# Softmax attention with 256-column products of P and V, and an output projection with two kept weight tiles and another order of PSUM banks

## The chip, the cores and the metric

One core of one Trainium2 chip. The metric is the device time of one execution in microseconds (us), lower is better. The unchanged kernel takes 2593.43 us, the median of 3 runs (2592.44 to 2593.51).

## The reference

Two layers over 1040 frames (16 learned ones and 1024 inputs) of width 1024. In each layer a normalised input goes through one projection into a group of linear-attention heads (GLA) and a group of eight softmax heads (FoX). The two groups' outputs, 512 columns each, go through one output projection and are added to the residual; a gated feed-forward part with a short convolution follows. The two places that the change touches, cut to what is computed:

```python
logits = einsum('bqhd,bkhd->bhqk', q_b, kf) + c_b[..., None] - c_k[:, :, None, :]
logits = where(key_pos <= q_pos, logits, -inf)
o = einsum('bhqk,bkhd->bqhd', softmax(logits, axis=-1), vf)          # FoX, per block of queries
...
h = h + concatenate([o_gla, o_fox], axis=-1) @ w_out[i]              # output projection
h = h + conv_ffn(rms_norm(h, ffn_norm[i]), ...)
```

## The kernel before

Activations lie transposed: eight tiles of 128 channels by 1040 frames. Every large product is made three times (`mm3`, L214): operand and weight are each split into a high part (rounded by a cast on ScalarE) and a low part (the difference, on VectorE), and high·high, low·high and high·low are summed in PSUM. A weight tile is loaded and split by `weights` (L170): for each four blocks of 128 rows one load on SP's queue (L179), one cast on ACT (L185) and one subtraction on DVE (L187; on POOL while the attention runs).

**Softmax attention.** Queries and keys are cut into nine tiles, the first of 112 frames and the others of 116 (`rows_of`, `start_of`). The work goes in steps of one head and one query tile; query tiles are grouped (7, 8), (5, 6), (3, 4), (1, 2), (0). A step makes scores S (L654, L655), the row maximum on DVE (L657) and P by an exponential on ACT (L669). Two steps later P is transposed on PE (L690), four key tiles to a PSUM tile `tr`, and split into PT (ACT L332, DVE L333). When both query tiles of a group are there, `fox_av` (L693) multiplies: V of one key tile, high and low part beside each other, is the weight (128 columns), and the two query tiles of PT, 2 x 116 = 232 columns, are what streams through; a key tile that only the later query tile sees has 116 columns. PT is stored as key tile, high or low part, 232 queries. Between the steps PE is given products of other projections as filler (`Work`); the tile framework's scheduler then orders each engine's list.

**Output projection.** The first four of the eight output tiles get seven eighths of their sum as filler of the attention. The rest is done in `ffn_up` by `wout` (L1098), where PE's order is the program's: for each half h of the frames (520 columns, in two products of 260) eight positions i, at each one output tile m out of `orders` (L1079). For h = 1 the tiles are 0, 4, 1, 5, 2, 6, 3, 7. Tiles 0 to 3 need one block of 128 rows (6 products), tiles 4 to 7 all eight (48 products). `stream` (L206) splits each position's weights while the position before is multiplied; so the weights of tiles 4 to 7 are loaded and split twice, once in each half. The sums lie in PSUM pairs of banks p0 to p3, taken by i % 4. DVE reads each sum out (L1110) and adds the residual, ACT squares it, DVE sums the squares (L1117). In the second half the scale of the first half is made after position 1: PE adds up the squares in p3 (`ssq`, L1086), DVE reads p3 (L1089), ACT and DVE form a reciprocal root (L273 to L277). The scaled first half is then written as operands x of the up projection (L1094, cast L1052, difference L1053) on the same two engines. `ensure` (L1071) splits the first five weight operands of the up projection (L1028, L1029) at the last position of h = 1. The up projection `up` follows, with sums and differences of operands; the second half's scale (again `ssq` in p3) stands after its first block of products.

Of the kernel before, what the change touches and what calls it, by code (L numbers as in the profile page):

```python
# [11 lines left out]
F32R = mybir.dt.float32r  # L12
# [12 lines left out]
KD = D // 128  # L25
# [8 lines left out]
FT, NT, FIRST = 116, 9, 112  # L34
# [5 lines left out]
M_GK, M_GQ, M_GV, M_GR, M_REM, M_FQ, M_FK, M_FV, M_WO, M_UP = 0, 2, 4, 8, 12, 13, 17, 21, 25, 33  # L40
# [11 lines left out]
NSPLIT = 4  # L52
# [82 lines left out]
class Kern:  # L135
# [31 lines left out]
        return self.vec[rows, o:o + 1]  # L167


    def weights(self, src, slots=None):  # L170
        nc = self.nc
        nk = src.shape[1]
        parts = []
        if slots:
            HI, LO = slots
        for k0 in range(0, nk, 4):
            n = min(4, nk - k0)
            raw = self.wp.tile([128, 4, 128], F32, tag="raw", name="raw", bufs=4)
            nc.sync.dma_start(raw[:, :n, :], src[:, k0:k0 + n, :])  # L179
            if slots:  # L180
                hi, lo = HI[:, k0:k0 + 4, :], LO[:, k0:k0 + 4, :]
            else:
                hi = self.wp.tile([128, 4, 128], F32R, tag="hi", name="hi")
                lo = self.wp.tile([128, 4, 128], F32R, tag="lo", name="lo")
            nc.scalar.copy(hi[:, :n, :], raw[:, :n, :])  # L185
            eng = nc.gpsimd if self.att else nc.vector
            eng.tensor_tensor(out=lo[:, :n, :], in0=raw[:, :n, :], in1=hi[:, :n, :].bitcast(F32), op=ALU.subtract)  # L187
            for k in range(n):
                parts.append((hi[:, k, :], lo[:, k, :]))
        return parts  # L190
# [485 lines left out]
    def fox_transposes(self, i, ci, P, PT, qoff, pp):  # L676
        nc = self.nc
        rows = self.rows_of(i)
        id_ = self.ident[:rows, :rows]
        tr = pp.tile([128, 4, 128], F32, tag="S" if ci == 2 else "tr", name="tr")  # L680
        qs = slice(qoff, qoff + rows)
        if ci == 2:
            nc.tensor.transpose(tr[:FT, 0, :FT], P[:FT, :FT], id_)
            self.split(PT[2][:, 0, :], PT[2][:, 1, :], tr[:FT, 0, :FT])
            return
        nt = min(4 * ci + 4, i + 1) - 4 * ci
        for j in range(nt):
            t = 4 * ci + j
            o, w = self.start_of(t) - self.start_of(4 * ci), FT if i else FIRST
            nc.tensor.transpose(tr[:w, j, :rows], P[:rows, o:o + w], id_)  # L690
        self.split(PT[ci][:w, :nt, 0, qs], PT[ci][:w, :nt, 1, qs], tr[:w, :nt, :rows])

    def fox_av(self, e, tiles, q, PT, avs, pp, part):  # L693
        nc = self.nc
        if part == 0:
            PT["av"] = pp.tile([128, 256], F32, tag="av", name="av")
        av = PT["av"]
        last = tiles[-1]
        width = FT * (len(tiles) - 1) + self.rows_of(last)
        for t in range(4 * part, min(4 * part + 4, last + 1)):  # L700
            a = 0 if t <= tiles[0] else FT
            for i in range(2):
                if t == NT - 1:
                    w, x = q["Vm"][:, e, :, :], PT[2][:, i, :]
                else:
                    r = self.rows_of(t)
                    w, x = q["V"][e][:r, t, :, :], PT[part][:r, t - 4 * part, i, a:width]
                nc.tensor.matmul(av[:, a:width], w.rearrange("p a b -> p (a b)"), x,  # L708
                                 start=(t == 0 and i == 0), stop=(t == last and i == 1))
        if last < 4 * part + 4:  # L710
            nc.scalar.copy(avs[:, e, :width], av[:, :width])

# [115 lines left out]
    def fox_schedule(self, lyr, at, n, p, e, ti, i, tiles, Ps, st, q, ap, pp, mix3):  # L828
        PT = st[e]

        def T_(ci, P):
            def f():
                if ti == len(tiles) - 1 and ci == 0:
                    for key in range(2):
                        PT[key] = ap.tile([FT, 4, 2, 2 * FT], F32R, tag=f"PT{key}", name=f"PT{key}", bufs=1)
                    if i == NT - 1:
                        PT[2] = ap.tile([FT, 2, FT], F32R, tag="PT2", name="PT2", bufs=1)
                self.fox_transposes(i, ci, P, PT, FT * ti, pp)
            return f
        for ci, P in enumerate(Ps):  # L840
            at(n + 2, f"T{ci}", T_(ci, P))
        if ti == len(tiles) - 1:
            PT["nch"] = len(Ps)
        if ti:
            return

        def av(ci):
            def f():
                if e == 0 and ci == 0:
                    one = len(tiles) == 1  # L850
                    st["avs"] = ap.tile([128, 2, FT if one else 2 * FT], F32, tag="av1" if one else "avs",
                                        name="avs", bufs=1)
                self.fox_av(e, tiles, q, PT, st["avs"], pp, ci)
            return f

        def fold():
            st["on"] = self.fox_fold(tiles, st["avs"], st["den"], ap, pp)

        def store():
            self.fox_store(lyr, p, tiles, st["on"], ap, pp, mix3() if p == 3 else None)  # L860
        for ci in range(PT["nch"]):
            at(n + 3, f"av{ci}", av(ci))
        if e == 1:
            at(n + 4, "fold", fold)
            at(n + 6, "store", store)
# [166 lines left out]
    def ffn_up(self, lyr, mix, hT, pp, fw, halves, o0, during_last):  # L1032
        nc, s = self.nc, self.slots
# [4 lines left out]
        bank2 = lambda name, i: pp.tile([128, 2, 512], F32, tag=f"p{i}", name=name, bufs=1)  # L1038
# [32 lines left out]
        def ensure(i):  # L1071
            while len(ops) < min(i + AHEAD + 1, len(seq)):
                ops.append(self.up_operand(lyr, *seq[len(ops)], fw, raws, len(ops) % 2))
# [5 lines left out]
        orders = [(4, 0, 5, 1, 6, 2, 7, 3), (0, 4, 1, 5, 2, 6, 3, 7)]  # L1079
        diff = lambda k: half(dd[k // 2], k % 2)  # L1080

        def scale(h):

            ps, r = bank2("ssq", 3), acc[:, sl[h]]
            for c in range(2):
                nc.tensor.matmul(ps[:, c, :n], self.ones[:], acc[:, halves[h] + c * n:halves[h] + c * n + n],  # L1086
                                 start=True, stop=True)
            vv, y0, a = half(tmp[0], 0), half(tmp[0], 1), half(tmp[1], 0)
            nc.vector.tensor_scalar(out=two(vv), in0=used(ps), scalar1=1.0 / D, scalar2=EPS, op0=ALU.mult, op1=ALU.add)  # L1089
            self.rsqrt(r, vv, y0, a)  # L1090
# [7 lines left out]
        def wout(i, h):  # L1098
            m = orders[h][i]
            k0 = KD - 1 if m < NSPLIT else 0  # L1100

            def f(w):
                if h == 1 and i == KD - 1:
                    ensure(0)
                ps = bank2("wo", i % 4)
                for k in range(len(w)):
                    for c in range(2):
                        self.mm3(ps[:, c, :n], w[k], mix[k0 + k], halves[h] + c * n, n, k == 0, k == len(w) - 1)
                x = hT[m][:, sl[h]]
                nc.vector.tensor_tensor(out=two(x), in0=used(ps), in1=two(x), op=ALU.add)  # L1110
                nc.gpsimd.dma_start(self.hm[m][:, sl[h]], x)
                if i == 0:
                    nc.scalar.activation(acc[:, sl[h]], x, AF.Square)
                else:
                    t = half(sq, i % 2)
                    nc.scalar.activation(t, x, AF.Square)
                    nc.vector.tensor_tensor(out=acc[:, sl[h]], in0=acc[:, sl[h]], in1=t, op=ALU.add)  # L1117
                if h == 0:
                    return
                if m < NSPLIT:  # L1120
                    nc.scalar.mul(half(gt, m % 2), x, gain(m))
                else:
                    nc.vector.scalar_tensor_tensor(out=diff(m - 4), in0=x, scalar=gain(m), in1=half(gt, m % 2),
                                                   op0=ALU.mult, op1=ALU.subtract)
                if i == 1:
                    scale(0)
                    operand(1)
                    operand(2)
                for k in turn.get(i, ()):
                    first_operand(k)  # L1130
            return (self.wm[lyr, M_WO + m][:, k0:KD, :], f)
        self.stream([wout(i, h) for h in range(2) for i in range(KD)])
        for x in mix:
            s.put(*x)
        s.put(gt)
# [93 lines left out]
        for i, (j, p) in enumerate(seq):  # L1229
# [3 lines left out]
            q = st.setdefault(j, {})  # L1233
# [3 lines left out]
            ps, w = q[bank], ops[i]  # L1237
# [452 lines left out]
```

## Time and profile before

| | |
|---|---|
| median of 3 runs | 2593.43 us |
| the profiled execution | 2591.4 us, of which the span is 2589.6 us |
| mean granted TensorE clock | 0.992 |
| busy share of the span | PE 96%, DVE 69%, ACT 50%, POOL 17% |
| products of P and V (`av`), layer 0, layer 1: first start, last start | 197.0, 524.1 us; 1474.1, 1800.8 us |
| products of the output projection in `ffn_up` (`wo`), layer 0, layer 1 | 538.9, 600.7 us; 1815.5, 1879.0 us |

The profile is of one execution. Times count from the start of the span. A row of the timeline has start, duration, engine, line, operation, what is written and read, and in brackets the idle time before it and what ended that. A matmul's duration has the way through the array in it, so the spacing of starts is what a product costs in a row of products. A row of the windows has, for one stretch, its length, each engine's busy time and number of instructions, the granted clock (PEclk), the DMA share and GB/s. A group row has busy time, mean ns of one, and idle time before. A row of the waits has total us, times, and the longest.

### The profile page before, as it was taken

How to read it: one execution, taken by the hardware profiler on the slowest of the kernel's cores; microseconds unless marked ns; L12 is line 12 of the kernel's file. 1: busy time of each engine (PE TensorE's matmuls, PEld its weight loads, DVE VectorE, ACT ScalarE, POOL GpSimd, SP SyncE). 2: the span in 40 equal slices, each digit the busy share in tenths (PEclk: the TensorE clock that was granted, in tenths of full speed). 3: DMA queues.
4: the chain of work that ended last, by engine and by line, in shares of the span. 5: the costliest groups of instructions: out<-in, count | busy, mean ns of one | idle time of the engine just before them, and what ended most of it. 6: DMA issues, size and time to landing. Idle time of an engine off the chain costs nothing.

```text
span 2589.6 us, 48743 instructions
## 1 busy us (share of the span) xinstructions
PE 2495.7 (96%) x19278; PEld 2424.9 (94%) x19278; DVE 1786.6 (69%) x3494; ACT 1288.4 (50%) x2745; POOL 432.6 (17%) x598
## 2 busy tenths in 40 slices
PE   8999999898999999999999999999999999999997
PEld 7988999898999999999999899998899999999997
DVE  7656776759877777853665666776697777777535
ACT  7336666635544445641443565665464444455312
POOL 4033334310000000100301233332100000001002
PEclk9999999999999999999999999999999999999998
DMA  3132134342322223863312222143423222257721
GB/s 125 65 89 60 51 93 127 109 145 89 110 75 87 79 79 129 200 165 107 110 50 67 72 78 76 57 146 114 148 70 114 78 74 86 76 162 179 196 61 67
DMA packets 119670, 263.03 MB, mean 102 GB/s; under 512 B 15008, under 2 KB 32672, under 8 KB 119440
## 3 DMA queue, kind: packets, MB, share of 16 engines
q1 hardware_dynamic: 95136, 184.89, 22.8%
q0 software_dynamic: 22432, 72.71, 10.1%
q8 instruction: 151, 2.47, 0.4%
q10 hardware_dynamic: 1872, 2.31, 0.3%
q14 instruction: 79, 0.65, 0.1%
HBM read 179.26 MB, written 67.81 MB: 95 GB/s over the span
## 4 chain that ended last, share of the span: by engine, by line
PE 62%; issue 16%; DVE 13%; ACT 4%; DMA 3%; POOL 1%; SPq 0%; DVEq 0%; POOLq 0%; ACTq 0%
PE mm L218 7%; PE mm L220 6%; PE mm L219 6%; PE up L218 5%; PE up L219 5%; PE up L220 5%; PE down L218 5%; PE down L219 5%; PE down L220 5%; PE av L708 2%; DVE S L657 2%; PE tr L690 2%; ACT P L669 1%; PE wo L218 1%; PE wo L219 1%
## 5 line engine op out<-in xcount | busy, mean ns | idle before, releaser
L218 PE MATMUL up<-x,hi 128*128 128x260 f32 (+1 forms) x2464 | 697.3, 283 | 2.3 <-ACT x L1052 1.6
L220 PE MATMUL up<-x,hi 128*128 128x260 f32 (+1 forms) x2464 | 695.8, 282 | 2.2 <-DVE x L1053 2.2
L219 PE MATMUL up<-x,lo 128*128 128x260 f32 (+1 forms) x2464 | 696.1, 283 | 0.8 <-DVE lo L1029 0.8
L220 PEld LDWEIGHTS up<-x,hi 128*128 128x128 f32 x2464 | 465.5, 189 | 3.1 <-DVE x L1053 3.1
L218 PEld LDWEIGHTS up<-x,hi 128*128 128x128 f32 x2464 | 464.4, 188 | 3.4 <-ACT x L1052 2.2
L219 PEld LDWEIGHTS up<-x,lo 128*128 128x128 f32 x2464 | 464.8, 189 | 1.0 <-DVE lo L1029 1.0
L1029 DVE TENSOR_TENSOR lo<-raw,hi 128x512 fp32r<-128x512 f32 x364 | 249.0, 689 | 171.3 <-ACT hi L1028 171.3
L218 PE MATMUL mm<-xh,hi 128*128 128x348 f32 (+4 forms) x1056 | 364.6, 345 | 0.0
L220 PE MATMUL mm<-xl,hi 128*128 128x348 f32 (+4 forms) x1056 | 340.1, 322 | 0.0
L219 PE MATMUL mm<-xh,lo 128*128 128x348 f32 (+4 forms) x1056 | 339.2, 321 | 0.0
L1028 ACT CAST hi<-raw 128x512 fp32r<-128x512 f32 x364 | 224.5, 620 | 145.0 <-PE up L220 87.4
L185 ACT CAST hi<-raw 128x512 fp32r<-128x512 f32 (+2 forms) x192 | 112.4, 587 | 201.4 <-PE down L220 114.2
L218 PEld LDWEIGHTS mm<-xh,hi 128*128 128x128 f32 x1056 | 200.2, 190 | 5.9 <-issue 5.3
L219 PEld LDWEIGHTS mm<-xh,lo 128*128 128x128 f32 x1056 | 200.1, 190 | 0.4 <-issue 0.3
L220 PEld LDWEIGHTS mm<-xl,hi 128*128 128x128 f32 x1056 | 198.9, 188 | 0.3 <-issue 0.3
L219 PE MATMUL down<-ah,lo 128*128 128x260 f32 (+1 forms) x704 | 198.6, 282 | 0.3 <-DVE lo L187 0.3
L220 PE MATMUL down<-al,hi 128*128 128x260 f32 (+1 forms) x704 | 198.3, 282 | 0.0
L218 PE MATMUL down<-ah,hi 128*128 128x260 f32 (+1 forms) x704 | 198.3, 282 | 0.0
L669 ACT ACTIVATE P<-S,m 116x460 f32<-116x460 f32 (+2 forms) x224 | 124.8, 561 | 100.1 <-DVE m L657 97.9
L333 DVE TENSOR_TENSOR PT<-tr,PT 116x464 fp32r<-116x464 f32 (+3 forms) x240 | 123.0, 516 | 63.2 <-ACT PT L332 62.3
L1222 POOL DMA_DIRECT2D actd<-cv x44 | 23.6, 535 | 763.5 <-DVE cv L1221 742.5
L1011 DVE TENSOR_TENSOR raw<-raw,raw 128x512 f32<-128x512 f32 x198 | 129.9, 689 | 22.4 <-DMA raw<-in_wd_dram 18.4
(276 smaller groups left out, 5901.0 us busy)
## 6 DMA issues: line engine op xcount, KB each, us to landing
raw<-in_wm_dram SPq DMA_DIRECT2D x338, 256.0 KB, 2.8
raw<-in_wd_dram SPq DMA_DIRECT2D x64, 256.0 KB, 3.5
actd<-cv POOLq DMA_DIRECT2D x22, 520.0 KB, 3.0
actd<-cv POOLq DMA_DIRECT2D x22, 512.0 KB, 3.0
cb<-cd SPq DMA_DIRECT2D x16, 520.0 KB, 3.8
st<-actd SPq DMA_DIRECT2D x14, 520.0 KB, 4.8
st<-actd SPq DMA_DIRECT2D x14, 512.0 KB, 5.3
kA<-kA SPq DMA_DIRECT2D x24, 260.0 KB, 4.3
```

Source lines behind the costliest of these rows:

```text
L185: nc.scalar.copy(hi[:, :n, :], raw[:, :n, :])
L218: nc.tensor.matmul(ps, wh, xh[:, c0:c0 + n], start=first, stop=False, skip_group_check=more)
L219: nc.tensor.matmul(ps, wl, xh[:, c0:c0 + n], start=False, stop=False, skip_group_check=more)
L220: nc.tensor.matmul(ps, wh, xl[:, c0:c0 + n], start=False, stop=last, skip_group_check=more)
L333: nc.vector.tensor_tensor(out=lo, in0=src, in1=hi.bitcast(F32), op=ALU.subtract)
L657: nc.vector.tensor_tensor_reduce(out=S[:rows, :n], in0=S[:rows, :n], in1=cb[:rows, c0:k1], scale=1.0, scalar=(BIG if ci == 0 else m[:rows, ...
L669: nc.scalar.activation(P[:rows, :n], S[:rows, :n], AF.Exp, scale=-1.0, bias=m[:rows, nch - 1:nch], accum_out=(den if nch == 1 else d3[:row ...
L690: nc.tensor.transpose(tr[:w, j, :rows], P[:rows, o:o + w], id_)
L708: nc.tensor.matmul(av[:, a:width], w.rearrange("p a b -> p (a b)"), x, start=(t == 0 and i == 0), stop=(t == last and i == 1))
L1011: nc.vector.tensor_tensor(out=q[out][:, :nk, :], in0=q[a][:, :nk, :], in1=q[b][:, :nk, :], op=op)
L1028: nc.scalar.copy(hi[:, :nk, :], src[:, :nk, :])
L1029: nc.vector.tensor_tensor(out=lo[:, :nk, :], in0=src[:, :nk, :], in1=hi[:, :nk, :].bitcast(F32), op=ALU.subtract)
```

## The change

1. `fox_av`: where both query tiles see a key tile and the tile isn't the first of its four, the product is made 256 columns wide; the 24 further columns of the sum aren't read. For this PT is stored as high or low part, key tile, query, with the four key tiles in reversed places, so that the 24 columns after a tile's 232 are those of the key tile before it. The first of four has no room behind it and stays at 232. The sum starts with key tile 1, which clears all 256 columns.
2. `weights` takes other tiles for its split parts (`keep`). In `wout` the split weights of output tiles 5 and 6 are kept from h = 0 to h = 1, in buffers of the up projection's pool (`raw2`, `hi2`, `lo2`).
3. The pairs of PSUM banks in h = 1 are 0, 1, 2, 0, 1, 3, 2, 1 by position.

```diff
@@ fox_transposes
-            nc.tensor.transpose(tr[:w, j, :rows], P[:rows, o:o + w], id_)
-        self.split(PT[ci][:w, :nt, 0, qs], PT[ci][:w, :nt, 1, qs], tr[:w, :nt, :rows])
+            nc.tensor.transpose(tr[:w, 3 - j, :rows], P[:rows, o:o + w], id_)
+        at = slice(4 - nt, 4)
+        self.split(PT[ci][:w, 0, at, qs], PT[ci][:w, 1, at, qs], tr[:w, at, :rows])
@@ fox_av
-        for t in range(4 * part, min(4 * part + 4, last + 1)):
-            a = 0 if t <= tiles[0] else FT
+        ts = list(range(4 * part, min(4 * part + 4, last + 1)))
+        if part == 0 and last:
+            ts[:2] = 1, 0
+        for t in ts:
+            a, b = 0 if t <= tiles[0] else FT, width
...
-                    r = self.rows_of(t)
-                    w, x = q["V"][e][:r, t, :, :], PT[part][:r, t - 4 * part, i, a:width]
-                nc.tensor.matmul(av[:, a:width], w.rearrange("p a b -> p (a b)"), x,
-                                 start=(t == 0 and i == 0), stop=(t == last and i == 1))
+                    r, p = self.rows_of(t), 3 - t % 4
+                    w, x = q["V"][e][:r, t, :, :], PT[part][:r, i, p, a:width]
+                    if a == 0 and p < 3:
+
+                        b = 256
+                        x = PT[part][:r, i].rearrange("p a b -> p (a b)")[:, 2 * FT * p:2 * FT * p + b]
+                nc.tensor.matmul(av[:, a:b], w.rearrange("p a b -> p (a b)"), x,
+                                 start=(t == ts[0] and part == 0 and i == 0), stop=(t == last and i == 1))
@@ fox_schedule
-                        PT[key] = ap.tile([FT, 4, 2, 2 * FT], F32R, tag=f"PT{key}", name=f"PT{key}", bufs=1)
+                        PT[key] = ap.tile([FT, 2, 4, 2 * FT], F32R, tag=f"PT{key}", name=f"PT{key}", bufs=1)
@@ ffn_up
-                ps = bank2("wo", i % 4)
+                ps = bank2("wo", (0, 1, 2, 0, 1, 3, 2, 1)[i] if h else i % 4)
...
-        self.stream([wout(i, h) for h in range(2) for i in range(KD)])
+        keep = {5: (fw, [("raw2", 7)] * 2), 6: (fw, [("hi2", 3), ("lo2", 3)])}
+        kept = {}
+
+        def wout_weights(h, i):
+            m = orders[h][i]
+            if m in kept:
+                return kept.pop(m)
+            w = self.weights(self.wm[lyr, M_WO + m][:, KD - 1 if m < NSPLIT else 0:KD, :], keep=keep.get(m))
+            if m in keep:
+                kept[m] = w
+            return w
+        todo = [(h, i) for h in range(2) for i in range(KD)]
+        ahead = wout_weights(*todo[0])
+        for this, nxt in zip(todo, todo[1:] + [None]):
+            w, ahead = ahead, nxt and wout_weights(*nxt)
+            wout(this[1], this[0])(w)
```

More of the change, by code (lines that the diff above doesn't have):

```diff
@@ L167, in v, with weights @@
         return self.vec[rows, o:o + 1]
-    def weights(self, src, slots=None):
+    def weights(self, src, slots=None, keep=None):
         nc = self.nc
@@ L181, in weights @@
                 hi, lo = HI[:, k0:k0 + 4, :], LO[:, k0:k0 + 4, :]
+            elif keep:
+                hi, lo = (keep[0].tile([128, 4, 128], F32R, tag=t, name="keep", bufs=b) for t, b in keep[1])
             else:
@@ L1130, in f @@
                     first_operand(k)
-            return (self.wm[lyr, M_WO + m][:, k0:KD, :], f)
-        self.stream([wout(i, h) for h in range(2) for i in range(KD)])
+            return f
+        keep = {5: (fw, [("raw2", 7)] * 2), 6: (fw, [("hi2", 3), ("lo2", 3)])}
[13 more added lines that the diff above has]
+            wout(this[1], this[0])(w)
         for x in mix:
```

## The prediction

> **What bounds the kernel now.** I read the page's first lines, then the windows around the two places of the change, then PE's waits there.
>
> ```profile
> span 2589.6 us, 48743 instructions
> PE 2495.7 (96%) x19278; PEld 2424.9 (94%) x19278; DVE 1786.6 (69%) x3494; ACT 1288.4 (50%) x2745; POOL 432.6 (17%) x598
> ```
> ```profile
> 189.00:530.00 341.00, 321.40 (x2248) 306.51 (x2247) 234.83 (x728) 213.08 (x638) 121.55 (x172) 0.99 0.28 85
> 530.00:571.00 41.00, 40.33 (x316) 39.82 (x315) 20.50 (x41) 13.85 (x28) 6.74 (x11) 1.00 0.60 177
> 571.00:608.00 37.00, 30.87 (x221) 29.86 (x221) 33.82 (x55) 20.49 (x36) 3.78 (x7) 0.91 0.36 118
> 608.00:647.00 39.00, 36.66 (x298) 35.64 (x298) 39.00 (x65) 23.41 (x43) 1.78 (x2) 1.00 0.27 76
> 650.00:700.00 50.00, 50.00 (x421) 50.00 (x420) 46.78 (x60) 27.41 (x38) 3.08 (x5) 1.00 0.35 115
> 1848.00:1885.00 37.00, 31.23 (x213) 30.27 (x212) 32.04 (x52) 19.45 (x35) 3.78 (x7) 0.86 0.34 117
> ```
>
> The columns after the length are PE, weight load, DVE, ACT and POOL, then the clock. Over the whole span PE bounds, and so it does in the attention of layer 0 (first row) and in the first half of the output projection (second row). The third row is the second half, h = 1: PE is busy for 30.87 of 37 us at a clock of 0.91, and DVE for 33.82. In the fourth row DVE is busy for all of 39.00 us. From 571 to 647 us, then, the end is set by DVE's list, which carries weight splits, read-outs, the scale and the operands of the up projection. From 650 us PE is full again, so what DVE gains before stays gained. Layer 1 (last row) looks the same, with a clock of 0.86. PE's own waits there (us in total, times, longest), first layer 0, then layer 1:
>
> ```profile
> PE wo L219 <- DVE lo L187: 3.7, 2, 3.2
> PE wo L218 <- DVE nt L1089: 1.9, 1, 1.9
> ```
> ```profile
> PE wo L219 <- DVE lo L187: 3.9, 2, 3.4
> PE wo L218 <- DVE nt L1089: 1.9, 1, 1.9
> ```
>
> The first of each is tiles 6 and 7 waiting for the low parts of their weights; the second is position 3 waiting until DVE has read `ssq` out of p3. After the idle times the clock falls:
>
> ```profile
> 576.30:579.70 3.40, 3.40 (x18) 3.40 (x17) 2.61 (x4) 1.19 (x3) 0.05 (x1) 0.50 0.59 155
> 593.40:596.80 3.40, 2.98 (x14) 2.98 (x14) 3.40 (x7) 1.73 (x4) 0.54 (x1) 0.50 0.54 182
> ```
>
> Each such stretch of 3.4 us at half clock costs PE 1.7 us.
>
> **The wider products.** By the loops, 14 products per head and part (6, 4, 3, 1 and 0 for the five groups) become 256 wide: 14 x 2 parts x 8 heads x 2 layers = 448 of the 640 that are 232 wide; the instruction list of the changed kernel has the same 448.
>
> ```profile
> 299.81 0.32 PE L218 MATMUL mm<-xh,hi 128*128 128x348 f32 x1
> ...
> 300.29 0.83 PE L708 MATMUL av<-PT,V 112*128 112x232 f32 x6
> 300.96 0.37 PE L654 MATMUL S<-kA,qA 128*116 128x460 f32 x1
> ```
> ```profile
> 2449.83 0.28 PE L219 MATMUL down<-ah,lo 128*128 128x256 f32 x1
> ...
> 2452.90 0.28 PE L218 MATMUL down<-ah,hi 128*128 128x256 f32 x1
> ```
>
> Six products of 232 columns (the row names the first one's form) take 300.96 - 300.29 = 0.67 us, 112 ns each. The 26 products of 256 between the last two rows take 3.07 us, 118 ns each. So one costs 6 ns more, and 448 cost 2.7 us, nearly all of it on PE's path, as PE is busy for 321.40 of 341 us there. The bounds: nothing, where the product ends before a wait; and from 256 to the 348 columns of the first row (three products in 0.48 us, 160 ns) a column costs (160 - 118) / 92 = 0.46 ns, so at most 24 x 0.46 = 11 ns each, 4.9 us. I take 2.7, as the 256-column row shows this very width with 128 weight columns. The stored order of PT changes no size of a cast or subtraction; the scheduler moves a few of them among their neighbours, which I put at nothing, with rival C as its price.
>
> The Trainium skill, page "TensorE: Matmul & The Clock Gate", section "LDWEIGHTS (loading the stationary operand)", gives the load of 128 weight columns as columns / 1.2 GHz, 107 ns, which is more than 232 columns at 2.4 GHz take and as much as 256 take. By it the widening would be free (rival D). The trace's 112 and 118 ns speak for a difference.
>
> **The output projection.** The kept tiles take away, per layer, four loads, four casts and four subtractions of 128x512 in h = 1. DVE's list from the read-out after position 1 on:
>
> ```profile
> 571.63 0.70 DVE L1110 TENSOR_TENSOR h<-wo,h 128x520 f32<-128x520 f32 x1 [1.48 <-PE wo L220]
> ...
> 574.22 0.69 DVE L1089 TENSOR_SCALAR nt<-ssq 128x520 f32<-128x520 f32 x1
> ...
> 576.28 0.70 DVE L275 SCALAR_TENSOR_TENSOR nt<-nt 128x520 f32<-128x520 f32 x1 [0.57 <-ACT nt L274]
> ...
> 580.26 0.69 DVE L187 TENSOR_TENSOR lo<-raw,hi 128x512 fp32r<-128x512 f32 x1 [1.32 <-ACT hi L185]
> ...
> 593.07 1.30 DVE L187 TENSOR_TENSOR lo<-raw,hi 128x512 fp32r<-128x512 f32 x2
> 594.27 0.70 DVE L1110 TENSOR_TENSOR h<-wo,h 128x520 f32<-128x520 f32 x1
> ...
> 605.62 0.70 DVE L1089 TENSOR_SCALAR nt<-ssq 128x520 f32<-128x520 f32 x1
> ...
> 608.16 0.69 DVE L275 SCALAR_TENSOR_TENSOR nt<-nt 128x520 f32<-128x520 f32 x1
> ```
> ```profile
> 1848.36 0.70 DVE L1110 TENSOR_TENSOR h<-wo,h 128x516 f32<-128x516 f32 x1 [1.50 <-PE wo L220]
> ...
> 1885.82 0.69 DVE L275 SCALAR_TENSOR_TENSOR nt<-nt 128x516 f32<-128x516 f32 x1
> ```
>
> Layer 0: between 571.63 and 605.62, 33.99 us, stand 52 instructions, 50 of full size, with 0.57 and 1.32 us of idle time; so one of full size takes about 0.63 us (two in a row stand 0.60 apart at 593.07). The list of the changed kernel has 46 of full size and one small one in the same stretch: three splits of tiles 5 and 6 are gone, one combination and the last x are later, and one split of the up projection is earlier. 46 x 0.63 + 0.2 = 29.2 us, and 0.4 for the exponential that still stands between L1089 and L275. The 1.32 goes: it was the wait for a cast of tile 6's weights, and there is no such cast in h = 1 any more. So the second L1089 starts about 4.4 us earlier, and with it the scale, all operands x after it and, as DVE is full to 647 us, PE's filled stretch. That the last x is late for PE is no loss yet: PE gets to it after the `ssq`, which waits for DVE as well.
>
> PE can follow this. Position 3 starts at once, since p0 was read long before; that takes out the 1.9. Position 5 uses p3, whose `ssq` is read out during position 3, and 7 uses p1, read out after position 4. Kept tiles don't wait. **What is late next:** the second half of tile 7's low part stands on DVE six instructions after the read-out of position 5 (6 x 0.63 + 0.69, done 4.5 us after it starts), and PE wants it after position 6 and half of tile 7, 30 products or 3.6 us after its last product of position 5, about 3 us after that read-out starts: about 1.5 us of waiting where it was 3.2. Then the `ssq` of the second half waits for DVE's sum of squares for nearly 3 us, after which the clock may fall once (1.7 us of PE). All this happens ahead of L1089's successors on DVE and costs at most 0.6 us more through a read-out that DVE waits for; it is in the range.
>
> Layer 1: the same stretch up to L275 takes 1885.82 - 1848.36 = 37.46 us against 608.16 - 571.63 = 36.53 in layer 0, since its clock and its waits were worse. With the list of layer 0 it should take 36.53 - 4.4 = 32.1, a gain of 5.3.
>
> Hidden edits: the kept tiles' three first subtractions now stand on DVE ahead of the last read-out that the projection's first product waits for:
>
> ```profile
> 538.26 0.57 DVE L961 TENSOR_TENSOR h<-mm,h 128x400 f32<-128x400 f32 x1 [3.18 <-PE mm L220]
> ```
>
> 3 x 0.63 = 1.9 us fit into its 3.18 of idle time; were the loads late, up to 1.9 us per layer would show. On SP the loads of the up projection's first operands move behind those of h = 0, and on POOL a summing DMA goes with them; the up projection needs them only after the last `wo` product, some 60 us later. The order of key tiles and the cleared columns cost no instruction.
>
> **Sum**, against the profiled execution (2591.4 us, 2.0 below the median of the runs shown): -4.4 - 5.3 + 2.7 = -7.0, that is 2584.4; on the median 2586.4.
>
> **Rivals.**
> A, PE decides and all its waits go: 3.7 + 1.9 + 2 x 1.7 in layer 0, and in layer 1 3.9 + 1.9 and (1 - 0.86) x 37 = 5.2 of clock, together 20.0, less 2.7: 2576.1. For it speaks that these are PE's waits; against it DVE's 39.00 of 39.00.
> B, new waits for PE on ACT: two casts of the up projection's operands now stand between the scaled operands and wait for buffers, one for the kept tile 6 (free in the middle of position 5), one for tile 3 (position 6). If they hold up ACT, and through it DVE's differences, by 2 us in each layer, 5.7 - 2.7 are left: 2590.4. Against it: by the count above PE is in position 5 when ACT gets to the first of them and in 6 when it gets to the second, so that each holds ACT up by 1 us at most.
> C, slower: in the attention PE stops at many places for PT:
>
> ```profile
> PE tr L690 <- DVE PT L333: 10.4, 10, 2.2
> ```
>
> Ten waits of 1.0 us in the mean in layer 0, as many in layer 1. The clock has stayed at 0.99 there, while the 1.9 us of the output projection brought the half clock. If the moved subtractions made such a stop longer, past some 1.9 us, it would cost the 0.9 and 1.7 of clock, 2.6 us. From three of the twenty (7.0 / 2.6) the change brings nothing, from five it is slower by over 0.2%; with eight it is 2586.4 + 8 x 2.6 = 2607.2. Against it: PE's order in the attention is nearly the old one. (The Trainium skill, same page, section "What's actually happening", has the clock fall after an idle window of about 3.4 us; by that, C could not be. The 0.50 row after 1.9 us of idle time says that less is enough.)
> D, the widening is free, because each of these products is bound by its weights: 2583.7. Against it: the products of 256 have weights of the same size, and take 118 ns.
>
> **How the numbers follow.** Forecast 0.46 (by itself 2582 to 2590: the bounds of 0 and 4.9 for the widening, 0.6 per layer for the clock, 1 for layer 1); A 0.09, B 0.22, C 0.10, D 0.13. The range, 2579.5 to 2592.5, leaves out A and most of C. About 0.2%, 5.2 us, is what a measurement of this kernel can tell from no change. Faster, below 2588.2: most of the forecast (0.41), A and D: 0.63. Slower, above 2598.6: C, 0.10. The rest, 0.27, is the same.
>
> **What would show it.** The products of PV start 118 ns apart, and the attention of layer 0 is about 1.3 us longer. PE's wait for L1089 is gone; that for the low part of tile 7 is near 1.5; one for the sum of squares has come, near 3. DVE is full from 580 to 643 us, and the second L1089 follows the read-out after position 1 by 29.6 us instead of 33.99. I am wrong if DVE has idle time there (B), if PE fills up well before 643 us (A), or if the attention grows by several us (C).

## The result and the profile after

The changed kernel takes 2573.96 us, the median of 4 runs (2572.21 to 2578.22), against 2593.47 us for the kernel before (4 runs, 2592.44 to 2598.25): a ratio of 0.9919, with a 95% interval of 0.9905 to 0.9932, or 17.6 to 24.6 us less. The forecast was 7.0 us less. The sign was right and the size was not; of its two terms, +2.7 us for the attention and -9.7 us for the output projection, the first was wrong in sign too, as the experiments show.

The page of the changed kernel, first its span and busy times, then the group of exponentials:

```profile
span 2570.4 us, 48719 instructions
PE 2498.7 (97%) x19278; PEld 2426.8 (94%) x19278; DVE 1780.0 (69%) x3486; ACT 1280.0 (50%) x2737; POOL 431.8 (17%) x598
L672 ACT ACTIVATE P<-S,m 116x460 f32<-116x460 f32 (+2 forms) x224 | 124.9, 561 | 79.2 <-DVE m L660 75.4
```

The same group on the page of the kernel before:

```profile
L669 ACT ACTIVATE P<-S,m 116x460 f32<-116x460 f32 (+2 forms) x224 | 124.8, 561 | 100.1 <-DVE m L657 97.9
```

PE is busy for 3.0 us longer in a span that is 19.2 us shorter. ACT does the same 224 exponentials in the same 561 ns each, but stands idle before them for 79.2 us instead of 100.1; nearly all of that idle time ends with a row maximum `m` from DVE (97.9 us before, 75.4 now). That is in the attention, where nothing was to be gained by the forecast. The windows of the changed kernel say the same (columns as in the prediction):

```profile
189.00:530.00 341.00, 329.97 (x2284) 314.25 (x2283) 236.88 (x737) 214.78 (x645) 121.12 (x172) 0.99 0.28 86
571.00:608.00 37.00, 33.45 (x259) 32.48 (x258) 36.17 (x59) 19.92 (x35) 3.64 (x6) 0.95 0.33 104
608.00:647.00 39.00, 36.68 (x283) 35.45 (x282) 36.95 (x57) 24.24 (x39) 1.79 (x2) 0.96 0.30 82
1848.00:1885.00 37.00, 32.32 (x248) 31.46 (x247) 35.43 (x58) 20.41 (x36) 1.73 (x4) 0.95 0.24 77
```

In the attention of layer 0 PE has gone from 321.40 to 329.97 busy of 341 us, and 36 more products fall into the window. PE's waits there (us in total, times, longest), in the kernel before for layer 1 too, since the prediction shows only layer 0's wait for PT:

```profile
PE S L654 <- ACT P L669: 5.7, 5, 1.5
...
PE tr L690 <- DVE PT L333: 10.1, 9, 2.2
PE S L654 <- ACT P L669: 5.7, 5, 1.6
```

and in the changed kernel, layer 0 and then layer 1:

```profile
PE tr L693 <- DVE PT L336: 3.8, 5, 2.2
PE S L657 <- ACT P L672: 3.0, 5, 1.5
PE S L657 <- DVE ml L339: 1.4, 1, 1.4
...
PE tr L693 <- DVE PT L336: 4.9, 6, 2.2
...
PE S L657 <- DVE ml L339: 1.7, 1, 1.7
PE S L657 <- ACT P L672: 1.6, 4, 0.8
```

Waits for PT and P went from 10.4 + 5.7 to 3.8 + 3.0 us in layer 0 and from 10.1 + 5.7 to 4.9 + 1.6 in layer 1, which is 18.6 us less. One wait in each layer is new, 1.4 and 1.7 us for the low part `ml` of a finished head's output, so that some 15.5 us of this waiting are gone.

**One such stop, before.** DVE, then ACT, then PE, in the kernel before:

```profile
281.14 0.15 DVE L732 TENSOR_TENSOR fv<-fv,fd 112x2 f32<-112x2 f32 x1
...
281.80 0.16 DVE L275 SCALAR_TENSOR_TENSOR fa<-fy 112x2 f32<-112x2 f32 x1 [0.43 <-ACT fy L274]
...
282.38 0.34 DVE L617 TENSOR_SCALAR ge<-gx 128x348 f32<-128x348 f32 x1 [0.23 <-DMA mixd<-ge]
...
283.03 0.64 DVE L657 CUSTOM_DVE_ANT_0 S<-S,cb 116x460 f32<-116x460 f32 x1
```
```profile
282.75 0.49 ACT L618 ACTIVATE ge<-ge 128x348 f32<-128x348 f32 x1 [0.99 <-DVE ge L617]
283.28 0.59 ACT L619 ACTIVATE gy<-ge,ones 128x348 f32<-128x348 f32 x1
283.90 0.49 ACT L620 ACTIVATE gy<-gy 128x348 f32<-128x348 f32 x1
284.30 0.53 ACT L332 CAST PT<-tr 116x464 fp32r<-116x464 f32 x1
284.72 0.65 ACT L669 ACTIVATE P<-S,m 116x460 f32<-116x460 f32 x1
```
```profile
285.51 0.46 PE L654 MATMUL S<-kA,qA 128*116 128x460 f32 x1 [1.53 <-ACT P L669]
```

The row maximum `S<-S,cb` (L657) stands on DVE behind the tiny operations (`fv`, `fa`, L732 and L275) of the fold, which normalises the output of heads that are finished, and behind `ge`, the gate that multiplies the linear heads' output. DVE waits there twice, 0.43 us for ACT's answer `fy` and 0.23 us for a DMA. So the maximum starts at 283.03, by which time ACT has begun the gate's three exponentials (L618 to L620), and P comes behind them and behind PT's cast, at 284.72. PE wants a score bank that P still holds and stands for 1.53 us.

**The same place after**, again DVE, ACT and PE:

```profile
279.06 0.15 DVE L743 TENSOR_TENSOR fv<-fv,fd 112x2 f32<-112x2 f32 x1
279.13 0.63 DVE L660 CUSTOM_DVE_ANT_0 S<-S,cb 116x460 f32<-116x460 f32 x1
...
279.72 0.16 DVE L278 SCALAR_TENSOR_TENSOR fa<-fy 112x2 f32<-112x2 f32 x1
```
```profile
279.59 0.53 ACT L335 CAST PT<-tr 116x464 fp32r<-116x464 f32 x1
280.48 0.50 ACT L621 ACTIVATE ge<-ge 128x348 f32<-128x348 f32 x1 [0.36 <-DVE ge L620]
281.01 0.59 ACT L622 ACTIVATE gy<-ge,ones 128x348 f32<-128x348 f32 x1
281.50 0.63 ACT L672 ACTIVATE P<-S,m 116x460 f32<-116x460 f32 x1
...
282.12 0.48 ACT L623 ACTIVATE gy<-gy 128x348 f32<-128x348 f32 x1
```
```profile
282.27 0.47 PE L657 MATMUL S<-kA,qA 128*116 128x460 f32 x1 [0.24 <-ACT P L672]
```

Now the row maximum stands right behind `fv`, in the time in which DVE waited for ACT before; `fa` doesn't wait any more. On ACT the cast of PT stands ahead of the gate's exponentials and P ahead of the last of them. PE waits 0.24 us instead of 1.53. Between 223 and 409 us the attention of layer 0 had six stops of 1.0 to 1.5 us, two of this kind and four for PT. In the changed kernel none of 0.5 us or more stands between 203 and 449 us.

Nothing in the diff orders this. The scheduler lists each engine's instructions when the program is built, and with products of 256 columns the lists of the two attentions come out otherwise: 212 places of DVE's list, 149 of ACT's, 244 of PE's, 4 of POOL's and 6 of SP's hold another instruction. (The traces, which name an instruction only by its operation, tiles and sizes, show 196 places of DVE's list and 143 of ACT's changed.) With 232 columns and everything else of the attention part, they are the lists of before.

### The profile page after: what moved, and what is told of

Read it like the earlier page. It is cut to its first block, busy times and chain, and to the rows that moved or that the text cites. A ratio compares the mean times of both kernels' runs of the same rounds, so it can differ in the third digit from the quotient of the medians.

```text
span 2570.4 us, 48719 instructions
## 1 busy us (share of the span) xinstructions
PE 2498.7 (97%) x19278; PEld 2426.8 (94%) x19278; DVE 1780.0 (69%) x3486; ACT 1280.0 (50%) x2737; POOL 431.8 (17%) x598
## 3 DMA queue, kind: packets, MB, share of 16 engines
q0 software_dynamic: 22432, 72.71, 10.2%
## 4 chain that ended last, share of the span: by engine, by line
PE 62%; issue 16%; DVE 12%; ACT 5%; DMA 3%; POOL 1%; SPq 0%; DVEq 0%; POOLq 0%; ACTq 0%
PE mm L221 6%; PE mm L222 6%; PE mm L223 6%; PE up L222 6%; PE up L223 6%; PE up L221 6%; PE down L221 5%; PE down L222 5%; PE down L223 5%; PE av L719 2%; DVE S L660 2%; PE tr L693 2%; ACT P L672 1%; PE S L657 1%; DVE PT L336 1%
## 5 line engine op out<-in xcount | busy, mean ns | idle before, releaser
L188 ACT CAST hi<-raw 128x512 fp32r<-128x512 f32 (+2 forms) x176 | 102.2, 582 | 196.8 <-PE down L223 115.6
L672 ACT ACTIVATE P<-S,m 116x460 f32<-116x460 f32 (+2 forms) x224 | 124.9, 561 | 79.2 <-DVE m L660 75.4
L1022 DVE TENSOR_TENSOR raw<-raw,raw 128x512 f32<-128x512 f32 x198 | 129.3, 684 | 20.8 <-DMA raw<-in_wd_dram 18.1
```

The lines of the kernel that those rows point to most:

```text
L672: nc.scalar.activation(P[:rows, :n], S[:rows, :n], AF.Exp, scale=-1.0, bias=m[:rows, nch - 1:nch], accum_out=(den if nch == 1 else d3[:row ...
L1022: nc.vector.tensor_tensor(out=q[out][:, :nk, :], in0=q[a][:, :nk, :], in1=q[b][:, :nk, :], op=op)
```

## The experiments

Two theories. **ORDER**: the new lists take PE's waits away, and the width costs what the prediction said. **WIDTH**: wide products, or the layout that they need, are better on the chip. The twelve kernels were timed in three groups of four, each group beside the kernel before on a chip of its own (att_only, att_narrow, att_254 and wo_only against a median of 2597.24 us; narrow_new, wide_old, mix_dve and mix_pe against 2596.56; the rest against 2596.44). The last column is the ratio's distance from 1, times that median:

| kernel | ratio to before, 95% interval | us against before |
|---|---|---|
| att_only: attention part | 0.9935, 0.9923 to 0.9947 | -16.9 |
| att_narrow: the same, 232 columns | 1.0006, 0.9995 to 1.0016 | +1.6 |
| att_254: the same, 254 columns | 1.0006, 0.9995 to 1.0018 | +1.6 |
| wide_old: 256 columns, lists of before | 0.9999, 0.9989 to 1.0010 | -0.3 |
| narrow_new: 232 columns, lists of after | 0.9945, 0.9928 to 0.9962 | -14.3 |
| mix_dve: 232 columns, DVE's list of after | 0.9960, 0.9946 to 0.9974 | -10.4 |
| mix_pe: 232 columns, PE's list of after | 0.9989, 0.9977 to 1.0001 | -2.9 |
| wo_only: output projection's part | 0.9966, 0.9956 to 0.9976 | -8.8 |
| wo_keep: kept tiles alone | 0.9974, 0.9965 to 0.9983 | -6.8 |
| wo_bank: bank order alone | 0.9989, 0.9980 to 0.9997 | -2.9 |
| after_232: after, 232 columns, its lists | 0.9907, 0.9887 to 0.9927 | -24.1 |
| after_rep: after once more | 0.9907, 0.9893 to 0.9920 | -24.1 |

**The two parts by themselves.** att_only is the changed kernel with `keep = {}` and the banks by `i % 4`; wo_only is the kernel before with the changed `weights`, `wout` and banks.

> Before, with the attention part of the change alone (layout of PT, tile 1 ahead of tile 0, products 256 wide); the output projections are as before. Its lists of instructions in attention are those of the changed kernel. Theory ORDER (the 256-wide instruction makes the scheduler that lists the instructions at build time put row maxima, exponentials and the fold's small operations in another order, and that order takes waits of TensorE away): about -12 us, from the shift of -4.65 and -7.2 us that the two attentions show between the traces. Theory WIDTH (the wide products, or the layout, are themselves better on the chip): -12 us as well. My prediction's step (casts and subtractions moved at no cost, products 6 ns longer): +2.7 us.

> Before, with the output projection's part alone (kept weight tiles, banks in another order); attention as before. ORDER, with what the shifts between the traces show for the two output projections (-2.3 and -4.5): -6.8 us. My prediction's terms: -9.7 us.

Measured: -16.9 us (-20.0 to -13.8) and -8.8 us (-11.4 to -6.2). The attention part makes two thirds of the two together. The +2.7 that the prediction gave it lies far outside its interval, and the -12 that was read from two single executions lies outside too, short of it. The output projection's -9.7 lies inside its interval, and so does the -6.8 from the same two executions.

**Width without the lists.** The layout alone, and a product that is wide but two columns short of 256:

```diff
@@ att_narrow, fox_av
-                    if a == 0 and p < 3:
-
-                        b = 256
-                        x = PT[part][:r, i].rearrange("p a b -> p (a b)")[:, 2 * FT * p:2 * FT * p + b]
@@ att_254, fox_av
-                        b = 256
+                        b = 254
```

> The attention part with the new layout of PT and tile 1 first, but with products of 232 columns. The lists of instructions on every engine are those of the kernel before. ORDER: 0, within 1 us of before, and TensorE's waits for PT's subtraction near 10 us in each attention. A rival by which the layout (both halves of PT written in longer runs) is what helps: about -12 us.

> The attention part with products of 254 columns in place of 256. TensorE's list is that of the kernel before, VectorE's differs in 20 places, ScalarE's in 2. ORDER: the wide products at their price with the waits of before: 448 x 6 ns x 22/24 = +2.5 us (from +1 to +4). WIDTH: -10 us or more, since two columns fewer can hardly matter on the chip.

Both came out at 1.0006 and hold 1 within their intervals. So neither the layout nor 254 columns bring anything that these runs can tell from nothing. ORDER expects this, as both have the lists of before (att_254 but for a few places); for att_254 its +2.5 lies inside the interval as well.

For the other corners of the square the lists were set by hand: edges that order two instructions of one engine and make no wait on a semaphore.

```diff
+ORDER = {
+    "DVE": (
+        (2402, 2396, 2406, 2359, 2650, 2412),
...
+def ordered(tc):
+    info = mybir.DependencyInfo(mybir.DependencyClass.NoSync, mybir.DependencyReason.DATA)
+    for chains in ORDER.values():
+        for c in chains:
+            for x, y in zip(c, c[1:]):
+                tc.add_manual_dep(tc.nc.get_inst_by_name(f"I-{y}"), f"I-{x}", info, reason="order")
...
         tile_hybrid_trunk_kernel(tc, *args)
+        ordered(tc)
```

Each number is an instruction as the program issues it, which the narrow and the wide kernel share; with these edges all five lists are, instruction for instruction, those of the other kernel. The traces of PE, DVE, ACT and POOL show the same sequence in narrow_new as in att_only and in wide_old as in att_narrow, but for the width.

> The attention part with products of 256 columns, and the lists of all five engines set by hand to those of the kernel before. ORDER: only the price of the wide products is left, +2.7 us (0 to +4.9), and the ten waits for PT's subtraction and five for P in each attention are back. WIDTH: -12 us or more.

> The attention part with products of 232 columns, and the lists of all five engines set by hand to those of the attention part with 256 columns. ORDER: what the attention part alone gave (ratio 0.9935), and the price of the wide products saved on top: 448 x 6 ns = 2.7 us, ratio 0.9925 (0.991 to 0.994). WIDTH: 0.

Measured: 256 columns in the old order give -0.3 us (-2.9 to +2.6), 232 columns in the new order -14.3 (-18.7 to -9.9). The -14.3 was expected to be 2.7 us better than att_only's -16.9; the intervals overlap, and which of the two is faster isn't shown. The waits of PE in the attention of layer 0 go with the lists, not with the width. First wide_old, then narrow_new:

```profile
PE tr L693 <- DVE PT L336: 10.8, 8, 2.2
PE S L657 <- ACT P L672: 5.0, 5, 1.4
```
```profile
PE tr L693 <- DVE PT L336: 4.3, 6, 2.2
PE S L657 <- ACT P L672: 3.2, 5, 1.4
```

The time from the first score to the first product of the output projection in the traces, both layers added up, shows it once more. Old lists: 715.2 us in the kernel before, 724.9 in att_narrow, 717.6 in wide_old. New lists: 701.6 in att_only, 702.2 in narrow_new, 703.4 in the changed kernel, 701.4 in after_rep, 699.4 in after_232. The means are 719.2 and 701.6: 17.6 us for the order. (Four more traces whose attention has the old lists, or all but a few places of them, have 716.1, 717.6, 720.5 and 724.3: wo_only, wo_keep, wo_bank and att_254.) PE's idle time between the same two points averages 43.4 us with the three old lists and 25.5 with the five new ones, which is the whole difference.

**Which engine's list.** 

> The attention part with products of 232 columns; VectorE's list alone is set to that of the 256-column attention part, the other four engines keep the lists of before. If the row maxima that go ahead of the fold's small operations on VectorE are what takes the waits away: ratio near 0.995, half to three quarters of the gain. If ScalarE's list (the cast of PT ahead of the gate's exponentials) or TensorE's is what counts: within 3 us of before.

> The attention part with products of 232 columns; TensorE's list alone is set to that of the 256-column attention part, the other four engines keep the lists of before. ORDER, with VectorE and ScalarE as the place: within 2 us of before. If TensorE's own order is what counts: ratio near 0.994.

PE's list alone gives -2.9 us (-6.0 to +0.3), which reaches no change; PE's own order by itself matters little. DVE's alone gives -10.4 (-14.0 to -6.8), some 60% of the attention part's gain. The waits of mix_dve in layer 0, and ACT's rows at the stop of above, show what is left:

```profile
PE S L657 <- ACT P L672: 8.2, 7, 2.5
PE tr L693 <- DVE PT L336: 5.1, 4, 3.3
```
```profile
281.50 0.49 ACT L623 ACTIVATE gy<-gy 128x348 f32<-128x348 f32 x1
281.90 0.53 ACT L335 CAST PT<-tr 116x464 fp32r<-116x464 f32 x1
282.33 0.65 ACT L672 ACTIVATE P<-S,m 116x460 f32<-116x460 f32 x1
```

With the row maxima early the wait for PT halves, to 5.1, but that for P grows from 5.7 to 8.2: in ACT's old list P still stands behind the gate's exponentials and PT's cast. That ACT's new list brings the rest is argued from these rows, not shown: neither ACT's new list by itself nor DVE's and ACT's without PE's was run.

**The output projection in halves.** wo_keep is wo_only with the banks by `i % 4`, wo_bank is wo_only with `keep = {}`.

> Before, with the kept weight tiles 5 and 6 alone; PSUM banks of the output projection and the attention as before. If VectorE's list sets the end of the stretch, as the prediction has it: the four instructions of full size per layer and the idle 1.3 us go all the same, -6 to -9 us (ratio 0.9965 to 0.9977), nearly all of what both edits together gave (-8.7). If TensorE's waits set it: about half of that, since the wait for the read-out of the sum of squares (1.9 us and 1.7 us of half clock per layer) stays.

> Before, with the other order of PSUM banks alone. If VectorE's list sets the end: 0 to -2 us, since the list keeps its length and TensorE's saved wait of 1.9 us comes back at the next wait for the low parts of weights. If TensorE's waits set it: -2 x (1.9 + 1.7) = -7 us (ratio 0.9972).

The kept tiles give -6.8 us (-9.1 to -4.4), the banks -2.9 (-5.2 to -0.8). The first lies where DVE's list as the bound puts it (-6 to -9), the second a little beyond its 0 to -2, though well short of the -7 that PE's waits as the bound would give. A part of PE's 1.9 us per layer may thus be saved for good: in wo_bank's trace the stretch that took 33.99 us before takes 31.77, where the eight traces with this projection unchanged have 32.58 to 34.96. In layer 1 the difference isn't clear (32.27 against 31.05 to 34.98).

**A version without the wide products.**

> The changed kernel with products of 232 columns in place of 256 and the lists of all five engines set by hand to those of the changed kernel. ORDER: everything the change gave, and the price of the wide products saved: 2.7 us (0 to 4.9) below the changed kernel run beside it.

> The changed kernel itself, for a comparison on the same chip as the run with 232 columns: ratio to before 0.992, as in the result; or 0.9901, the product of the two parts run alone (0.9935 and 0.9966), if the parts add up without loss.

The two can't be told apart: 2571.45 and 2572.01 us, with ratios whose intervals reach 0.002 and 0.0013 to each side. The 2.7 us expected for the width can't be told from nothing here, so after_232 doesn't beat the changed kernel measurably; it shows that the gain needs no wide product once the order is set.

## Why the prediction failed, step by step

**The step that failed** is this sentence of the widening's part: "the scheduler moves a few of them among their neighbours, which I put at nothing, with rival C as its price". In its place the square of width and lists shows that the new order is worth -14.3 us at the old width (and 17.6 us in the traces), and the width in the old order -0.3. So the attention's term was wrong in sign and size. Rival C had the right place, the stops for PT, and looked at one sign only: that they could grow. Its counter-argument, that PE's order is nearly the old one, speaks of PE's list, which by itself is worth little (mix_pe), and says nothing of the lists of DVE and ACT, which release PE. The quoted row, ten waits of 1.0 us, was also a sum that could be won, and the 5.7 us in each layer in which PE waits for P weren't looked at.

**The widening's price** was right per product. In the changed kernel:

```profile
207.97 0.98 PE L719 MATMUL av<-PT,V 116*128 116x256 f32 x7
208.79 0.26 PE L693 MATMUL tr<-ident,P 116*116 116x116 f32 x1
```

The seven take 0.82 us. Two of them, of the first key tile, are still 232 wide; at the 112 ns of before they take 0.22, which leaves 0.60 us for the five wide ones, 119 to 120 ns each. That is near the 118 predicted. Of what 448 of them cost the path, the attentions with the new lists show 702.1 us in the mean of three with 256 columns against 700.8 of two with 232: 1.3 us, within the bounds of 0 and 4.9 and less than these executions differ among themselves. Rival D, that width is free, has its premise against it; its number, nothing, the times can't exclude (wide_old: -2.9 to +2.6). (The Trainium skill, page "TensorE: Matmul & The Clock Gate", section "LDWEIGHTS (loading the stationary operand)", would, by an estimate from its rule for 128 columns, bind both widths to the same 107 ns; 112 and 119 ns speak against it once more.)

**The output projection** was right in its mechanism. The DVE rows of the changed kernel that answer to 571.63 and 605.62, and in layer 1 to 1848.36 and 1885.82, and PE's waits, layer 0 and then layer 1:

```profile
565.85 0.70 DVE L1121 TENSOR_TENSOR h<-wo,h 128x520 f32<-128x520 f32 x1 [2.20 <-PE wo L223]
...
595.15 0.70 DVE L1100 TENSOR_SCALAR nt<-ssq 128x520 f32<-128x520 f32 x1 [0.31 <-PE ssq L1097]
...
1833.95 0.70 DVE L1121 TENSOR_TENSOR h<-wo,h 128x516 f32<-128x516 f32 x1 [2.19 <-PE wo L223]
...
1866.41 0.69 DVE L278 SCALAR_TENSOR_TENSOR nt<-nt 128x516 f32<-128x516 f32 x1
```
```profile
PE ssq L1097 <- DVE r L1128: 2.6, 1, 2.6
PE wo L222 <- DVE lo L190: 1.0, 1, 1.0
...
PE ssq L1097 <- DVE r L1128: 2.5, 1, 2.5
PE wo L222 <- DVE lo L190: 2.2, 1, 2.2
```

The stretch takes 29.30 us (29.6 predicted, 33.99 before). In layer 1 the one that was to take 32.1 us, up to the first row of the reciprocal root, takes 32.46 (37.46 before). The wait for the read-out of the squares is gone, that for tile 7's low part is 1.0 and 2.2 (1.5 predicted), the new one for the sum of squares 2.6 and 2.5 ("nearly 3"). DVE is no longer full to 647 us, 36.95 of 39.00, as ACT holds it up for 1.1 us and PE for 1.0, so that its list no longer sets the end alone. As a term, layer 0 was nearly right: from the first product of the output projection to the 800th of the up projection, the five traces of before, att_narrow, att_254, wide_old and att_only average 163.8 us and the four with the new projection (wo_only, the changed kernel, after_rep, after_232) 159.9: -3.9 for -4.4. Layer 1 looks oversized: 164.4 and 161.6, -2.8 for -5.3 (with narrow_new, mix_dve and mix_pe, which have the old projection too, layer 0 stays at -3.9 and layer 1 comes to -2.2). The base for it was the one execution of before, whose clock in that window was 0.86, with 10.2 us of half clock in the whole projection of layer 1. wide_old has as much there, the six other traces with the old projection between 0 and 6.8 us. The timed -8.8 of wo_only can't decide it: both -6.7 and -9.7 lie inside its interval.

**Rivals A and B.** A held that PE's waits in the output projection and the half clock behind them all go; the wait for the read-out of the squares is gone, the waits for low parts and the half clock are still there in part. That A's 2576.1 lies nearest to the measured time is chance: the output projection alone brought 8.8 us, where A has 20.0. B's 2 us for DVE behind ACT didn't come: in the stretch of 29.30 us, the one idle time of DVE behind its first row is the 0.31 us for PE, and from there to 647 us ACT holds DVE up for 1.1 us.

**The sum.** +2.7 - 9.7 = -7.0 was forecast; -16.9 and -8.8, the two parts alone, make -25.7, and both together gave, by their ratios, -21.0 and -24.1 in two groups of runs (17.6 to 24.6, and 20.8 to 27.8 less). The parts add up within what these runs can tell. The attention's term is off by 19.6 us, more than the whole error, and the output projection's by 0.9.

## What to carry to other kernels

Where a framework's scheduler orders the engines, an edit that changes an instruction's shape can change every list around it: set the old and new lists of the engines that release the bound one against each other, and price the moved instructions at the waits that recur, with both signs. A row of ten waits of the same kind is a sum that an order may win; look at what stands ahead of the releasing instruction on its engine, above all at operations that wait there for another engine. A gain of a change is told apart from its by-product only by giving each without the other, here by the order at the old width and the width in the old order.

## What the runs showed of the hardware

The same wait brought half clock in one execution and not in another. The changed kernel's sum of squares waits until 593.01 us, and the window behind it has a clock of 0.50:

```profile
592.90:596.20 3.30, 3.19 (x10) 2.81 (x11) 2.99 (x6) 1.56 (x3) 0.00 (x0) 0.50 0.10 36
```

In after_rep, the same program, the same wait of 2.58 us stands, and the clock stays full:

```profile
591.53 1.15 PE L1097 MATMUL ssq<-r,ones 128*128 128x260 f32 x4 [2.58 <-DVE r L1128]
```
```profile
591.40:594.70 3.30, 3.17 (x23) 3.06 (x24) 3.30 (x7) 1.91 (x4) 0.00 (x0) 1.00 0.11 38
```

So a wait of some 2 us costs 1.7 us more in some executions only. The kernel before shows it too: a stop of 2.20 us in its attention ends at 480.40 us, and the clock is 0.50 from 480.7 to 484.1; wide_old has two such stops, and no half clock near them. The Trainium skill, page "TensorE: Matmul & The Clock Gate", section "What's actually happening", has the clock judged over free-running windows of 3413 ns, so that it matters where in a window the wait falls. The trace agrees in so far as the stretches of half clock in its records are 3.41 us long or twice that (but for the one with which each trace ends), but the row of 2.58 us says that less than a full idle window can do it. It is one reason why executions with the same lists differ: the attention of layer 0 takes 353.2 us in the changed kernel, with one such stretch, and 350.6 in after_rep, with none. It is also why a term read from one execution, as layer 1's was, should be checked against a second stretch of the same kind.
